# Seven block products for all of one feed-forward layer, and weight sums moved from DMA to VectorE

## The chip, the cores and the metric

The kernel runs on one core of a Trainium2 chip. The metric is the device time of one execution in microseconds (us). A core has TensorE (PE; its weight loads are shown apart as PEld), VectorE (DVE), ScalarE (ACT), GpSimd (POOL) and SyncE (SP), and 16 DMA engines that serve all queues. In this kernel SP issues nearly all loads and stores, and POOL issues DMAs that add one DRAM array to another and the gathers of the paged cache.

## The reference

The reference is one inference step of a two-layer decoder for 1024 prompt tokens and 8 sample tokens that share all weights. The width is 1024 and the feed-forward width `D_FF` is 2816. Layer 0 mixes tokens with a gated linear recurrence beside cross-attention into 256 memory tokens; layer 1 mixes them with stick-breaking attention (over keys and values projected once, after layer 0) beside the same kind of memory attention. Each layer ends with a SwiGLU feed-forward block, and a normalisation stands around every block:

```python
def swiglu(h, w_gu, w_down):
    gate, up = jnp.split(h @ w_gu, 2, axis=-1)
    return (jax.nn.silu(gate) * up) @ w_down

h = h + rmsnorm(mix, g[1])
h = h + rmsnorm(swiglu(rmsnorm(h, g[2]), w_gu[l], w_down[l]), g[3])
```

Everything is float32. The outputs are the activations of all tokens, the recurrence's states, and the new keys and values.

## The kernel before

**Tokens and tiles.** Activations lie transposed: 8 tiles of 128 features by the tokens. There are two token groups: group 0 has 512 prompt tokens, group 1 has 512 prompt tokens and the 8 sample tokens (520 columns, worked on as two halves of 260). "Second half" below means group 1. A float32 product is made as three products of rounded pieces: each weight tile and each activation is split into a high part (a cast on ACT, `split_w` L206 and `split` L501) and a low part (a subtraction on DVE, L207 and L502), and high by high, high by low and low by high are added in PSUM.

**Feed-forward.** `D_FF` is cut into 22 slices of 128, in five parts, `PARTS` = 5, 5, 4, 4, 4 slices. A part makes its slices (gate product, up product, SiLU, multiplication, split), and then the part's share of the down product for 8 blocks of rows, added to the result. The slices exist in three forms:

- `ffn.part` (L684): gate and up are two full products through `proj` (L220). For group 1 a slice is 2 x 8 x 3 x 2 = 96 matmuls of 260 columns. SiLU is made of exp, ln and exp on ACT (L238 to L240).
- `gate_up_q` (L452, "plain"): the same 96 matmuls into four single PSUM banks Q0 to Q3, while the generator `sums_w` (L279) makes sums and differences of the activations' blocks between them. These are on DVE, with a split on ACT and DVE after each.
- `gate_up_w` (L482, "seven products"): gate and up for two token halves are a 2 x 2 block product, made by a Winograd-form scheme with 7 block products instead of 8: 7 x 4 x 3 = 84 matmuls of 260 columns (L511). Its seven weight operands are four blocks of `w_gu` and three further sums of them. Between the products ACT copies a negated bank into the next one (L518, L521), so that the order pa, pd, pb, pa, pb, pc, pb of the banks matters.

The sums of weight blocks are made in DRAM ahead of use by `weight_sums` (L549): per part four arrays s1 to s4, in 16 steps (two row halves of eight), each a DMA from POOL's queue that copies (L568) or adds (L566). Ahead of each stands a one-column copy on POOL (L563) that waits for a recent result named by `now[0]`; it holds the DMA back to that point of the program.

Class `ffn_w` (L575) runs parts with `gate_up_w`; its first three slices are plain ones, in which the activation sums come about. Layer 0 group 1 uses `ffn.part` for parts 0 and 1 (10 slices) and `ffn_w` from part 2 on (3 plain, 9 with seven products). Layer 1 group 1, the last work of the kernel, uses `ffn_w` for all five parts (3 plain, 19 with seven products).

**Order.** The kernel's main line (from L1535 on) is a list of stages. `weave` interleaves generators by weights (how far each has come of its expected count of steps). A scheduler then puts the instructions of the built program into the order in which each engine issues them; engines take their own list strictly in that order. The stages named below, in the time of the profiled run:

- 185 to 290 us: group 0's recurrence beside the memory keys and values.
- 672 to 852 us: the rest of group 1's layer-0 mixer beside group 0's layer-0 feed-forward parts 2 to 4.
- 990 to 1209 us, called the attention stage here: `b0.sb` and `b0.mem` (group 0's layer-1 attention: 12 steps of stick-breaking and 8 of memory attention) beside parts 0 and 1 of group 1's layer-0 feed-forward. 34 steps of layer 1's weight sums run in it too.
- 1209 to 1404 us: parts 2 to 4 of that feed-forward, alone.
- 1600 to 1920 us: group 1's layer-1 attention, prompt and sample, beside group 0's layer-1 feed-forward.
- 2067 to 2407 us, called the final stage here: group 1's layer-1 feed-forward, beside group 0's last output in its first 60 us.

The attention writes its result into eight tiles `xo` (`wo_tiles`), as high and low parts (`split_to` at the end of `sb_prompt` and `mem_attn`); the output projection `o0.mm(b0.xo, ...)` reads them after the feed-forward of group 1 has ended.

**Buffers.** Raw weight tiles come from `wraw` (5), in seven-product parts by turns from other pools as well; split weights come from `wspl` (5), and in part from `cpool`. `tpool` has 3 tiles, `mpool` 5.

Of the kernel before, what the change touches and what calls it, by code (L numbers as in the profile page):

```python
# [18 lines left out]
P = 128  # L19
# [4 lines left out]
def tile_decoder(  # L24
# [204 lines left out]

    def silu(dst, ps, g):  # L230


        n = NG[g]
        x = T()
        dst = T() if dst is None else dst
        d = dst[:, :n]
        nc.vector.tensor_scalar(sv(x, g), pv(ps, g), -44.0, None, op0=ALU.max)  # L237
        nc.scalar.activation(d, x[:, :n], AF.Exp, scale=-1.0)  # L238
        nc.scalar.activation(d, d, AF.Ln, bias=1.0)
        nc.scalar.activation(d, d, AF.Exp, scale=-1.0)  # L240
        nc.vector.tensor_mul(d, d, x[:, :n])
        return dst
# [36 lines left out]
    def sums_w(g, xs, ops, YT, ZT):  # L279
# [5 lines left out]
        for k in range(4):  # L285
            x0, x1 = xs[k], xs[k + 4]
            y = YT()
            if k % 2 == 0:
                z, u = ZT(), ZT()
            o = (k % 2) * h  # L290
            ops.append([
                x0[:, :, :h], x1[:, :, :h], x1[:, :, h:n], z[:, :, o : o + h], u[:, :, o : o + h],
                y[:, :, :h], y[:, :, h : 2 * h],
            ])

            def full(x, c):
                t = B()
                nc.vector.tensor_add(t[:, :h], x[:, 0, c : c + h].bitcast(F32), x[:, 1, c : c + h].bitcast(F32))
                return t

            b11, b12, b21, b22 = full(x0, 0), full(x0, h), full(x1, 0), full(x1, h)
# [150 lines left out]
    def gate_up_q(g, l, f, xt, side, n_side, first):  # L452
# [4 lines left out]
        for j in range(2):  # L457
# [14 lines left out]
            for a in range(2):  # L472
                d = sg[:, a * h : (a + 1) * h]
                if j == 0:
# [7 lines left out]
    def gate_up_w(g, l, f, ops, spl, raws):  # L482
# [5 lines left out]
        src = [  # L488
# [16 lines left out]
        def product(ps, j, first=False):  # L505
            w = split(weight(j))
            i = src[j][1]
# [16 lines left out]
        nc.scalar.activation(sg[:, :h], pa[:, :h], AF.Silu)  # L524
        product(pb, 4)
        dt = T()
        nc.scalar.copy(dt[:, h:n], pd[:, :h])
        gt = T()
        nc.vector.tensor_add(gt[:, h:n], dt[:, h:n], pb[:, :h])
        product(pc, 5)  # L530
        nc.vector.tensor_sub(gt[:, :h], pc[:, :h], dt[:, h:n])
        product(pb, 6)
        act[0] = nc.scalar.activation(sg[:, h:n], gt[:, :h], AF.Silu)
# [41 lines left out]
    class ffn_w:  # L575


        def __init__(self, g, l, x, steps, first, rows, R=None, own=False):
# [3 lines left out]
            self.half = []  # L582

            def YT():
                if rows:
# [5 lines left out]
            self.sums = sums_w(g, x, self.ops, YT, YT if rows else lambda: A(F32R))  # L591

        def spl(self):
            self.n += 1
            if (self.pi or not self.rows) and not self.own and self.n % 8 in (1, 4, 6):
# [9 lines left out]
        def raws(self):  # L605
            self.r += 1
            if not self.rows and self.r % 2:
# [8 lines left out]
        def part(self, pi):  # L616
# [5 lines left out]
            for j in range(nf):  # L622
                self.pi = pi
                if f0 + j < self.plain:
                    mids.append(
                        gate_up_q(g, l, f0 + j, self.x, self.sums, self.steps[j], PARTS[self.first][0])
                    )
                    now[0] = mids[-1][:, 0, 0:1].bitcast(F32)
                else:
                    mids.append(gate_up_w(g, l, f0 + j, self.ops, self.spl, self.raws))  # L630
# [233 lines left out]
    def mem_attn(g, l, qm, xo):  # L864
# [4 lines left out]
        for h in range(H):  # L869
# [41 lines left out]
            d = xo[H + h]  # L911
            split_to((d[:, 0, :G], d[:, 1, :G]), po)
# [427 lines left out]
    def sb_prompt(g, Qs, xo):  # L1340
# [49 lines left out]
        for h in range(H):  # L1390
# [13 lines left out]
            d = xo[h]  # L1404
            split_to((d[:, 0, :G], d[:, 1, :G]), po)
# [18 lines left out]
    class mixer_b:  # L1424
# [7 lines left out]
        def open(self):  # L1432
            self.xo = wo_tiles(self.g)
# [41 lines left out]
    with tc.issue_after(made[0].ins):  # L1475
# [60 lines left out]
    weave((a0.fq(), 8), (mem_load(), 2))  # L1536
    weave(
        (a0.core(), 22),
# [5 lines left out]
    w0 = weight_sums(0, (3, 4, 2))  # L1544
    weave((a0.mem(), 8), (a1.fq(), 8), (islice(w0, 12), 13))
    o0 = out_proj(0, 0, M)
    drain(o0.mm(a0.xo))
    weave((o0.finish(), 17), (chain(a1.v(), a1.qm(A)), 8), (islice(w0, 12), 13))
    f0 = ffn(0, 0, o0.x)
    weave((a1.core(), 22), (f0.part(0), 9), (islice(w0, 16), 17))  # L1550
    a1.open()
    weave((a1.sample(), 6), (a1.gate(), 4), (f0.part(1), 9), (w0, 9))
    ws = weight_sums(1, range(5))
# [10 lines left out]
    weave((chain(a1.merge(), a1.mem()), 30), (a1.mem_sample(), 50), (rest(), 24), (islice(ws, 2), 6))  # L1564
# [8 lines left out]
    weave((b0.heads(), 8), (o1.finish(), 17), (islice(ws, 4), 4))  # L1573
# [13 lines left out]
    weave((kv_proj(1, xk1), 8), (islice(ws, 10), 11))  # L1587
    weave((normed(1, f1.R, f1.r, lambda k: gcol(1, 0, k), xb1), 8), (o0.mm(b0.xo, 7, ND), 1))
    b1 = mixer_b(1, xb1)
    weave((b1.heads(), 8), (o0.finish(), 17), (islice(ws, 8), 9))  # L1590
# [8 lines left out]
    weave((o1.mm(b1.xo), 8), (ws, 9))  # L1599
# [37 lines left out]
```

## Time and profile before

| | |
|---|---|
| median of 3 runs | 2450.82 us (2448.91 to 2453.11) |
| the profiled execution | 2446.43 us, its span 2444.6 us |
| granted TensorE clock | 0.999 |
| PE busy | 2412.0 us, 99% of the span, 15839 matmuls |
| DVE busy | 1639.0 us, 67% |
| ACT busy | 1251.2 us, 51% |
| POOL busy | 186.1 us, 8% |
| DMA | 397.42 MB, of it 79.70 MB by POOL's queue |

The profile page gives, in this order, busy time by engine, the span in 40 slices, DMA queues, the chain of work that ended last, the costliest groups of instructions and the DMA issues. A row of a group reads: line, engine, operation, output<-inputs, shape, count | busy us, mean ns of one | idle time before them and what ended it. A row of a window reads: the stretch, its length, and each engine's busy us with its count of instructions, then the clock, the mean busy share of the DMA engines and GB/s. A row of the timeline reads: start us, length us, engine, line, operation, count, and in brackets idle time before it. The length of a matmul in the rows is the time from its start to its modelled end; matmuls overlap, so that length isn't their spacing.

### The profile page before, as it was taken

Reading aid. Unit: us, or ns where it says so; the run is one execution under the profiler, and the core shown is the slowest. Engines: PE = TensorE matmul, PEld = TensorE weight load, DVE = VectorE, ACT = ScalarE, POOL = GpSimd, SP = SyncE. Lnnn points to the kernel's source line nnn. Section 1 sums busy time; section 2 is a strip of 40 time slices with the busy share of each in tenths; the row PEclk is TensorE's granted clock in tenths of the full one; section 3 lists DMA queues with packets and bytes.
Section 4 is the critical chain, followed back from the end, with each engine's and each line's share of the span. In section 5 each row is a group of like instructions: output and inputs, shape, how many; then the busy total and the mean of one; then the engine's idle time right before and its main releaser. Section 6 shows DMA issues by size and latency. Waiting matters only on the chain.

```text
span 2444.6 us, 42106 instructions
## 1 busy us (share of the span) xinstructions
PE 2412.0 (99%) x15839; PEld 2159.3 (88%) x15839; DVE 1639.0 (67%) x2987; ACT 1251.2 (51%) x2441; POOL 186.1 (8%) x315
## 2 busy tenths in 40 slices
PE   8999999999999999999999999999999999999998
PEld 6888888888889988999999989877777888999998
DVE  5867557665897686654756686777788467755565
ACT  5547544344445555554434554555555445654445
POOL 1001101101000000111200102121000100000000
PEclk9999999999999999999999999999999999999999
DMA  5454666577746447677766649655354563464542
GB/s 187 120 166 117 161 191 158 134 192 186 209 132 172 123 156 232 179 179 168 196 166 165 202 139 293 196 151 150 99 163 121 145 192 119 140 193 144 148 145 73
DMA packets 534734, 397.42 MB, mean 163 GB/s; under 512 B 21325, under 2 KB 473018, under 8 KB 534530
## 3 DMA queue, kind: packets, MB, share of 16 engines
q1 hardware_dynamic: 505346, 315.02, 43.3%
q0 software_dynamic: 29184, 79.70, 14.1%
q8 instruction: 125, 2.05, 0.3%
q14 instruction: 79, 0.65, 0.1%
HBM read 364.81 MB, written 101.14 MB: 191 GB/s over the span
## 4 chain that ended last, share of the span: by engine, by line
PE 87%; DVE 6%; DMA 3%; issue 2%; ACT 2%; POOL 0%; SPq 0%; DVEq 0%; ACTq 0%; POOLq 0%
PE mm L220 46%; PE q L511 13%; PE q L648 9%; PE q L464 3%; PE mm L1042 2%; PE s L1188 1%; PE s L906 1%; PE s L1385 1%; PE mm L851 1%; PE mm L824 1%; PE s L875 1%; PE q L680 1%; PE s L1351 1%; DVE ws L207 1%; DMA b<-qd 1%
## 5 line engine op out<-in xcount | busy, mean ns | idle before, releaser
L220 PE MATMUL mm<-x,ws 128*128 128x260 f32 (+1 forms) x6240 | 1115.6, 335 | 3.5 <-DVE r L657 1.7
L220 PEld LDWEIGHTS mm<-x,ws 128*128 128x128 f32 x6240 | 941.0, 188 | 123.9 <-DVE x L228 2.1
L206 ACT CAST ws<-w 128x512 fp32r<-128x512 f32 (+1 forms) x652 | 382.3, 588 | 492.1 <-PE mm L220 336.2
L207 DVE TENSOR_TENSOR ws<-w,ws 128x512 fp32r<-128x512 f32 (+1 forms) x652 | 418.6, 648 | 246.0 <-ACT ws L206 232.0
L220 PE MATMUL mm<-m,ws 128*128 128x512 f32 (+1 forms) x1344 | 281.8, 361 | 0.5 <-DVE r L400 0.4
L220 PEld LDWEIGHTS mm<-m,ws 128*128 128x128 f32 x1344 | 217.8, 188 | 37.2 <-issue 1.0
L648 PE MATMUL q<-m,ws 128*128 128x260 f32 (+1 forms) x1824 | 222.0, 282 | 0.0
L648 PEld LDWEIGHTS q<-m,ws 128*128 128x128 f32 x1824 | 219.0, 188 | 1.3 <-DVE t L534 0.7
L502 DVE TENSOR_TENSOR ws<-w,ws 128x512 fp32r<-128x512 f32 x181 | 124.0, 690 | 89.7 <-ACT ws L501 86.3
L501 ACT CAST ws<-w 128x512 fp32r<-128x512 f32 x181 | 111.8, 621 | 110.8 <-PE q L648 31.9
L511 PE MATMUL q<-x,ws 128*128 128x260 f32 (+1 forms) x1188 | 158.1, 282 | 0.0
L511 PEld LDWEIGHTS q<-x,ws 128*128 128x128 f32 x1188 | 148.7, 188 | 0.0
L511 PE MATMUL q<-y,ws 128*128 128x260 f32 x912 | 119.7, 283 | 0.4 <-ACT q L521 0.4
L511 PEld LDWEIGHTS q<-y,ws 128*128 128x128 f32 x912 | 113.6, 188 | 0.9 <-ACT q L521 0.6
L464 PE MATMUL q<-x,ws 128*128 128x260 f32 (+1 forms) x720 | 91.3, 284 | 0.2 <-DVE r L400 0.2
L464 PEld LDWEIGHTS q<-x,ws 128*128 128x128 f32 x720 | 88.4, 188 | 1.8 <-DVE r L400 0.5
L511 PE MATMUL q<-a,ws 128*128 128x260 f32 (+1 forms) x672 | 87.0, 282 | 0.0
L511 PEld LDWEIGHTS q<-a,ws 128*128 128x128 f32 x672 | 83.2, 188 | 0.0
L657 DVE TENSOR_TENSOR r<-r,q 128x260 f32<-128x260 f32 (+1 forms) x128 | 48.4, 420 | 48.2 <-PE q L648 48.1
L237 DVE TENSOR_SCALAR t<-mm 128x512 f32<-128x512 f32 (+1 forms) x58 | 40.0, 690 | 48.6 <-PE mm L220 48.4
L563 POOL COPY mk<-a 128x1 f32<-128x1 f32 x36 | 21.9, 609 | 640.4 <-ACT a L1241 392.1
L566 POOL DMA_DIRECT2D wsum<-in_w_gu x64 | 58.5, 935 | 114.1 <-DMA wsum<-wsum 89.5
(355 smaller groups left out, 3027.8 us busy)
## 6 DMA issues: line engine op xcount, KB each, us to landing
w<-in_w_gu SPq DMA_DIRECT2D x297, 256.0 KB
w<-in_w_down SPq DMA_DIRECT2D x160, 256.0 KB
wsum<-in_w_gu POOLq DMA_DIRECT2D x72, 512.0 KB, 6.5
w<-wsum SPq DMA_DIRECT2D x104, 256.0 KB
w<-in_w_in_a SPq DMA_DIRECT2D x80, 256.0 KB
w<-in_w_o SPq DMA_DIRECT2D x64, 256.0 KB
wsum<-in_w_gu POOLq DMA_DIRECT2D x24, 640.0 KB, 6.8
wsum<-wsum POOLq DMA_DIRECT2D x24, 512.0 KB, 5.6
```

Of the source, the lines that this page charges most:

```text
L206: nc.scalar.copy(ws[:, 0, :n, :], raw[:, :n, :])
L207: nc.vector.tensor_sub(ws[:, 1, :n, :], raw[:, :n, :], ws[:, 0, :n, :].bitcast(F32))
L220: nc.tensor.matmul(ps[:, a, : PW[g]], wt, xt[k][:, xi, o : o + PW[g]], start=(k == 0 and wi == 0), stop=(k == nk - 1 and wi == 2),)
L237: nc.vector.tensor_scalar(sv(x, g), pv(ps, g), -44.0, None, op0=ALU.max)
L464: ins = nc.tensor.matmul(pp[a][:, :h], wt, xt[k][:, xi, a * h : (a + 1) * h], start=(k == 0 and wi == 0), stop=(k == ND - 1 and wi == 2),)
L501: nc.scalar.copy(w[:, 0, :], src)
L502: nc.vector.tensor_sub(w[:, 1, :], src, w[:, 0, :].bitcast(F32))
L511: nc.tensor.matmul(ps[:, :h], w[:, wj, k * P : (k + 1) * P], x[:, xi, :], start=(first and k == 0 and wi == 0), stop=(k == 3 and wi == 2), ...
L566: nc.gpsimd.dma_start(d, a, accum_op=ALU.add)
L648: nc.tensor.matmul(pp[a][:, :h], wt, mids[k][:, xi, a * h : (a + 1) * h], start=(k == 0 and wi == 0), stop=(k == nf - 1 and wi == 2),)
L657: nc.vector.tensor_add(d, d, pp[a][:, :h])
L1042: nc.tensor.matmul(pb[i][:, a, :], xt[k][:, xi, c * P : (c + 1) * P], ws[:, s, :], start=(k == 0 and wi == 0), stop=(k == ND - 1 and wi == 2),
```

## The change

1. Group 1's layer-0 feed-forward uses `ffn_w` from part 0 on: 3 plain slices and 19 with seven products, where it had 13 slices of 96 matmuls and 9 of 84. Parts 0 and 1 still run beside `b0.sb` and `b0.mem`, now in a form called `lean`: SiLU is again exp, ln, exp (`gated`) over all 520 columns at once. In these parts the raw tiles come from `wraw` and the split ones from `wspl` alone. The sums of activations read the normalised activations (`src=o1.R`) and no longer add high and low parts first.
2. The weight sums of layer 0 cover all five parts, in the order 3, 4, 0, 1, 2 (80 steps; 48 before). They start with the first mixer: 14 steps in the stage at 185 us, then 8, 6, 8 and 4, 24 in the stage at 672 us, and the last 16 in the attention stage.
3. Layer 1's weight sums in DRAM (80 steps) are gone. `gate_up_w` without them loads the four blocks of `w_gu` and makes the sums in SBUF with four `tensor_add` on DVE (128x512) per slice.
4. `b0`'s attention output goes to a DRAM array (`put`: a copy on ACT and a store), since the tiles that held it now hold activation sums. `b0.load` reads it back and splits it beside the last down product of that feed-forward.

```diff
+    def put(xo, i, cols, src):
+        if isinstance(xo, list):
+            split_to((xo[i][:, 0, cols], xo[i][:, 1, cols]), src)
+            return
+        t = B()[:, : cols.stop - cols.start]
+        nc.scalar.copy(t, src)
+        nc.sync.dma_start(xo[:, i, cols], t)
...
+            if src:
+                b11, b12, b21, b22 = (src[i][:, c : c + h] for i in (k, k + 4) for c in (0, h))
+            else:
+                b11, b12, b21, b22 = full(x0, 0), full(x0, h), full(x1, 0), full(x1, h)
...
+    def gated(d, x):
+        nc.scalar.activation(d, x, AF.Exp, scale=-1.0)
+        nc.scalar.activation(d, d, AF.Ln, bias=1.0)
+        nc.scalar.activation(d, d, AF.Exp, scale=-1.0)
+        nc.vector.tensor_mul(d, d, x)
...
         def weight(j):
-            r = raws()
-            nc.sync.dma_start(r, src[j][0].rearrange("(k p) m -> p k m", p=P))
-            return r.rearrange("p k m -> p (k m)")
+            if src:
+                return load(src[j][0])
+            if j == 0:
+                for name, r, c in (("a11", 0, gate), ("a21", 0, up), ("a22", 512, up), ("a12", 512, gate)):
+                    raw[name] = load(w_gu[l][r : r + 512, c : c + P])
+            elif j == 1:
+                raw["s1"] = B()
+                nc.vector.tensor_add(raw["s1"], raw["a21"], raw["a22"])
+            elif j == 2:
+                nc.vector.tensor_add(raw["a21"], raw["a11"], raw["a21"])
+                raw["s2"] = B()
+                nc.vector.tensor_add(raw["s2"], raw["a21"], raw["a22"])
+            elif j == 5:
+                nc.vector.tensor_add(raw["s2"], raw["s2"], raw["a12"])
+            return raw[("a11", "s1", "s2", "a12", "a21", "s2", "a22")[j]]
...
+        if lean:
+            nc.vector.tensor_scalar(sg[:, :h], pa[:, :h], -44.0, None, op0=ALU.max)
...
+            nc.scalar.copy(dt[:, :h], pd[:, :h])
+            nc.vector.tensor_add(gt[:, h:n], dt[:, :h], pb[:, :h])
+            product(pc, 5)
+            nc.vector.tensor_sub(sg[:, h:n], pc[:, :h], dt[:, :h])
+            nc.vector.tensor_scalar(sg[:, h:n], sg[:, h:n], -44.0, None, op0=ALU.max)
+            x, sg = sg, T()
+            product(pb, 6)
+            gated(sg[:, :n], x[:, :n])
...
         nc.vector.tensor_mul(sg[:, :h], sg[:, :h], pb[:, :h])
         nc.vector.tensor_mul(sg[:, h:n], sg[:, h:n], gt[:, h:n])
...
+        def load(self):
+            d, n, self.xo = self.xo, NG[self.g], []
+            ts = []
+            for k in range(ND + 2):
+                if k < ND:
+                    ts.append(T()[:, :n])
+                    nc.sync.dma_start(ts[k], d[:, k, :n])
+                if k >= 2:
+                    x = X(self.g)
+                    split_to((x[:, 0, :n], x[:, 1, :n]), ts[k - 2])
+                    self.xo.append(x)
+                yield
...
+    w0 = weight_sums(0, (3, 4, 0, 1, 2))
     weave(
-        (a0.core(), 22),
+        (a0.core(), 22), (islice(w0, 14), 15),
...
-    weave((chain(a1.merge(), a1.mem()), 30), (a1.mem_sample(), 50), (rest(), 24), (islice(ws, 2), 6))
+    weave((chain(a1.merge(), a1.mem()), 30), (a1.mem_sample(), 50), (rest(), 24), (islice(w0, 24), 24))
...
-    b0.open()
-    f1 = ffn(1, 0, o1.x)
-    weave((chain(b0.sb(), b0.mem()), 25), (chain(f1.part(0), f1.part(1)), 18), (islice(ws, 34), 35))
-    set_banks(True)
-    fw = ffn_w(1, 0, o1.x, (5, 6, 5), 2, False, f1.R)
-    weave((chain(fw.part(2), fw.part(3), fw.part(4)), 24), (islice(ws, 8), 8))
-    f1.acc = fw.acc
+    b0.open(True)
+    set_banks(True)
+    fw = ffn_w(1, 0, o1.x, (5, 6, 5), 0, False, beside=(0, 1), src=o1.R)
+    weave((chain(b0.sb(), b0.mem()), 25), (chain(fw.part(0), fw.part(1)), 18), (w0, 60))
+    p4 = fw.part(4)
+    weave((chain(fw.part(2), fw.part(3), islice(p4, 4)), 20))
+    weave((p4, 4), (b0.load(), 10))
+    f1 = ffn(1, 0, o1.x)
+    f1.R, f1.acc = fw.R, fw.acc
```

More of the change, by code (lines that the diff above doesn't have):

```diff
@@ L575, in tile_decoder, with __init__ @@
     class ffn_w:
-        def __init__(self, g, l, x, steps, first, rows, R=None, own=False):
+        def __init__(self, g, l, x, steps, first, rows, R=None, own=False, beside=(), src=None):
             self.g, self.l, self.x, self.ops, self.steps, self.rows, self.own = g, l, x, [], steps, rows, own
@@ L589, in YT @@
                 return A(F32R)
-            self.sums = sums_w(g, x, self.ops, YT, YT if rows else lambda: A(F32R))
+            self.sums = sums_w(g, x, self.ops, YT, YT if rows or beside else lambda: A(F32R), src)
         def spl(self):
             self.n += 1
-            if (self.pi or not self.rows) and not self.own and self.n % 8 in (1, 4, 6):
+            if (self.pi or not self.rows) and not self.own and self.pi not in self.beside and self.n % 8 in (1, 4, 6):
                 return cpool.tile([P, 2, 512], F32R, tag="c", name=nm("ws"))
@@ L606, in raws @@
             self.r += 1
-            if not self.rows and self.r % 2:
+            if not self.rows and self.pi not in self.beside and self.r % 2:
+                return B().rearrange("p (k m) -> p k m", k=4)
+            if self.rows and not self.pi and self.r % 2:
                 return B().rearrange("p (k m) -> p k m", k=4)
```

81 lines of the change are left out of this document (47 added, 34 removed).

## The prediction

> **What bounds the kernel now.** I read the page first: the engines' busy time, the clock, and the chain that ended last.
>
> ```profile
> span 2444.6 us, 42106 instructions
> PE 2412.0 (99%) x15839; PEld 2159.3 (88%) x15839; DVE 1639.0 (67%) x2987; ACT 1251.2 (51%) x2441; POOL 186.1 (8%) x315
> ...
> PEclk9999999999999999999999999999999999999999
> ...
> PE 87%; DVE 6%; DMA 3%; issue 2%; ACT 2%; POOL 0%; SPq 0%; DVEq 0%; ACTq 0%; POOLq 0%
> ```
>
> PE is busy for 99% of the span at the full clock and makes 87% of the chain. So the time moves with what PE has to do, and with the waits that an edit adds to PE. VectorE is next, at 67%. A matmul's length is no price here, since matmuls overlap; their spacing is. The timeline and the groups by shape show it:
>
> ```profile
> 2211.33 29.04 PE L648 MATMUL q<-m,ws 128*128 128x260 f32 x240
> ...
> 1486.98 5.99 PE L220 MATMUL mm<-x,ws 128*128 128x260 f32 x48
> ...
> L511 PE MATMUL q<-y,ws 128*128 128x260 f32 x912 | 119.7, 283 | 0.4 <-ACT q L521 0.4
> ```
>
> One matmul of 260 columns is 283 ns long, but 240 in a row take 29.04 us: (29.04 - 0.28)/239 = 0.120 us from start to start. The L220 run gives (5.99 - 0.28)/47 = 0.121. I price each at 0.120 us.
>
> Third, windows by stage, for how full the other engines are where the change puts work:
>
> ```profile
> 185.00:290.00 105.00, 103.92 (x669) 92.72 (x669) 69.65 (x133) 72.63 (x162) 11.59 (x24) 1.00 0.47 121
> 672.00:852.00 180.00, 177.88 (x1334) 166.40 (x1333) 136.60 (x269) 91.83 (x193) 0.76 (x2) 1.00 0.49 144
> 948.00:1003.00 55.00, 55.00 (x302) 46.27 (x303) 42.36 (x74) 30.36 (x53) 4.91 (x7) 1.00 0.85 238
> 990.00:1209.00 219.00, 218.35 (x1691) 207.96 (x1691) 133.26 (x262) 113.52 (x230) 34.56 (x65) 1.00 0.70 174
> 1384.00:1404.00 20.00, 20.00 (x168) 19.83 (x166) 14.15 (x27) 8.83 (x14) 1.21 (x2) 1.00 0.69 190
> 1600.00:1920.00 320.00, 313.70 (x1472) 241.26 (x1472) 247.18 (x389) 167.32 (x328) 22.13 (x20) 1.00 0.44 132
> 2103.00:2125.00 22.00, 21.57 (x178) 21.12 (x177) 15.97 (x32) 13.96 (x31) 0.00 (x0) 1.00 0.73 213
> 2311.00:2344.00 33.00, 33.00 (x277) 33.00 (x277) 21.71 (x39) 19.60 (x40) 0.00 (x0) 1.00 0.61 176
> ```
>
> After the stage's length come PE, PEld, DVE, ACT and POOL, then the clock and the DMA engines' share. In the attention stage (990 to 1209) PE idles 0.65 us; in the final stage not at all; in the stage with the fullest VectorE beside attention (1600 to 1920, DVE 247/320 = 77%) it idles 6.3 us, 2.0%.
>
> **The change, part by part.**
>
> *Matmuls.* Ten slices go from 96 to 84 matmuls: 120 fewer. The built program agrees: 8184 matmuls of 260 columns instead of 8304, all else on PE the same in number. 120 x 0.120 = 14.4 us off PE: 7 slices x 12 x 0.120 = 10.1 in the attention stage, and 4.3 in the stage behind it, whose three plain slices become seven-product ones. The Trainium skill, page "TensorE: Matmul & The Clock Gate", section "Back-to-back issue gap", puts the spacing at N/2.4 + 2.5 ns, which is 111 ns at 260 columns; by it the sum below would lose 1.1 us of its gain. The rows above say 120, and I keep them.
>
> *Work beside attention.* What VectorE gains and loses there:
>
> ```profile
> L237 DVE TENSOR_SCALAR t<-mm 128x520 f32<-128x520 f32 x10 | 7.0, 698 | 12.3 <-PE mm L220 12.3
> L241 DVE TENSOR_TENSOR t<-t,t 128x520 f32<-128x520 f32 x10 | 7.0, 700 | 12.4 <-ACT t L240 12.4
> L716 DVE TENSOR_TENSOR t<-t,mm 128x520 f32<-128x520 f32 x10 | 7.0, 696 | 15.3 <-PE mm L220 15.3
> L298 DVE TENSOR_TENSOR b<-x 128x260 f32<-128x260 f32 x16 | 6.3, 419 | 0.0
> ...
> L502 DVE TENSOR_TENSOR ws<-w,ws 128x512 fp32r<-128x512 f32 x17 | 11.8, 691 | 7.8 <-ACT ws L501 7.7
> L228 DVE TENSOR_TENSOR m<-t,m 128x520 fp32r<-128x520 f32 x3 | 2.1, 700 | 0.0
> L531 DVE TENSOR_TENSOR t<-q,t 128x260 f32<-128x260 f32 x4 | 1.7, 428 | 0.1
> ```
>
> Off: ten times L237, L241 and L716 (20.9 us), the 16 additions L298 (6.7), the eight subtractions of the attention's output (5.5, moved to the load). On: a seven-product slice splits 7 weight tiles instead of 4, so 21 x 0.69 = 14.5; ten products of `gated` at 0.70 (7.0); 54 operations of 260 columns, four in a plain and six in a seven-product slice, at 0.42 (22.7); two half additions for one whole in part 1's down product (1.2). Net +12 us: 145.6 of 209 us, 70%. ACT gains 21 casts of 0.62, 21 bank copies of 0.37 and 1 us of down copies, +22 us: 65%. So neither is the bound, but the chains are longer: a split tile lasts 12 matmuls instead of 24, from five buffers, and SP loads 7 tiles a slice instead of 4. Between the stages with DVE at 61% (idle 0.3%) and 77% (idle 2.0%), 70% gives 1.3% of 209, some 2 us more than the 0.65 now. I take +3, with -1 (that idle gone, and a little spacing) and +10.5 (the chain of the second case below, unhidden) as ends.
>
> *Weight sums on VectorE, final stage.* By lengths a seven-product slice now has 7 x 0.691 + 0.70 + 4 x 0.42 = 7.2 us on DVE beside 84 x 0.120 = 10.1 on PE; four additions of 0.69 make it 10.0. That looks full, but lengths overlap here too:
>
> ```profile
> 1322.09 1.28 DVE L502 TENSOR_TENSOR ws<-w,ws 128x512 fp32r<-128x512 f32 x2
> ...
> 1320.43 0.76 DVE L657 TENSOR_TENSOR r<-r,q 128x260 f32<-128x260 f32 x2 [0.99 <-PE q L648]
> ```
>
> Two subtractions take 1.28, so the second comes 0.59 after the first; for 260 columns 0.34. By spacing a slice needs 11 x 0.60 + 0.6 + 4 x 0.34 = 8.6 of 10.1 us, 85%, and catches up in each down product. I take +0.5 for 17 slices, and +1 for the two behind the window 2103 to 2125, where DVE has 16.0 of 22 already and 5.5 more come. Lower end 0, upper end the third case. That loads fall from seven to four a slice gains nothing: PE doesn't wait there.
>
> *Sums by DMA.* POOL issues 48 adding or copying steps fewer over all, each moved past its queue's waiting one-column copies; nothing else stands behind these but the sample gathers, which come later.
>
> ```profile
> q1 hardware_dynamic: 505346, 315.02, 43.3%
> q0 software_dynamic: 29184, 79.70, 14.1%
> ```
>
> 128 steps took at most 14.1% of 2444.6 us of all 16 engines: 2.7 us each. Fourteen in the stage at 185 lift its DMA share from 0.47 to 0.83, 22 more in the stage at 672 from 0.49 to 0.82. The window 948 to 1003 has 0.85 and no PE idle, so I charge +0.5 in all; ends 0 and +3 (the 1.1 and 2.1 us that PE idles in these two stages, doubled). In the attention stage 18 steps go (49 us) and 21 loads and 8 stores of 256 KB come, at 0.433 x 2444.6 us / 315 MB some 0.9 us each (26 us): its 0.70 falls to about 0.6. Nothing is gained for it.
>
> *Hand-over.* Eight tiles are read back and split beside the last down product. Its window (1384 to 1404) has DVE at 14.15 of 20; 8 x 0.69 = 5.5 more in 23.3 us makes 94%. PE already waits there once:
>
> ```profile
> 1404.93 2.33 PE L220 MATMUL mm<-x,ws 128*128 128x512 f32 x9 [0.90 <-DVE r L657]
> ```
>
> +1, ends 0 and +5.5 if the splits hide nowhere.
>
> *Sum.* -14.4 + 3 + 1.5 + 0.5 + 1 = -8.4 us. The profiled execution took 2446.43 us, so it would take 2438; it lies 4.4 under the median of the three runs, and 2450.8 - 8.4 gives 2442 for the median.
>
> **Rivals.**
>
> *The SiLU chain in the attention stage eats the gain.* `gated` works on both halves at once, so bank pb stays taken until the whole chain behind product 5 is done, and the next slice's third product needs pb.
>
> ```profile
> L238 ACT ACTIVATE t<-t 128x520 f32<-128x520 f32 x10 | 6.4, 641 | 0.9
> L886 ACT ACTIVATE b<-s,nmx 128x256 f32<-128x256 f32 x16 | 7.5, 472 | 6.6 <-DVE nmx L880 6.6
> ...
> L501 ACT CAST ws<-w 128x512 fp32r<-128x512 f32 x16 | 9.9, 621 | 5.3 <-PE q L511 3.8 <-ACT ws L501 1.5
> ...
> L518 ACT ACTIVATE q<-q 128x260 f32<-128x260 f32 x3 | 1.1, 372 | 0.6 <-PE q L511 0.6
> ```
>
> Subtraction and maximum 0.85, three ACT passes 1.92 with a cast (0.62) and two attention exponentials (0.94) among them, two products 1.12, the negated copy 0.37: 5.8 us. PE has products 6, 0 and 1 meanwhile, 36 x 0.120 = 4.3. That is 1.5 us a slice, 10.5 for seven, and with 3 in the final stage and 2 elsewhere the sum is +1: 2452, no change. For it: these chains are built into the order. Against it: PE has attention matmuls to put in that place, and now loses 0.65 us in 219.
>
> *VectorE bounds the final stage (slower).* If additions can't overlap, a slice costs 10.0 us on DVE plus the waits for ACT that its row L502 shows, 7.8 us in 3.3 slices, 2.4 each: 12.3 against 10.1, 19 x 2.2 = +42, and 2450.8 - 14.4 + 42 + 4.5 = 2483. It decides once a slice's DVE time passes 10.1. The two rows of overlapping pairs speak against it. The Trainium skill has the rule for it, page "VectorE: DVE Perf Modes", section "The DRAIN you can't avoid": the next operation cannot issue until the pipe is empty. The trace agrees with its page's length for such an addition (691 ns) but not with the rule, with 0.59 us between starts.
>
> *The earlier sums starve the loads.* If an eighth of the DMA time that joins the two early stages (36 x 2.7 = 97 us) shows up on PE, 12 us come back: -8.4 + 12 = +4, 2455. For it: the steps are let go by one-column copies that wait for few results, so they may come in bursts. Against it: the window with a share of 0.85.
>
> **How the numbers follow.** Forecast 0.58 (own range 2434 to 2447), SiLU chain 0.22, VectorE 0.12, loads 0.08. A measurement of this kernel tells about 0.2%, 4.9 us, from no change. Faster (under 2446): most of the forecast, 0.56. Same: the rest of it and most of the SiLU chain, 0.22. Slower: VectorE, the loads, and the chain at its worst, 0.22. The range leaves out the full VectorE case: 2433 to 2460.
>
> **What would show it.** PE's busy time should fall by about 14 us and its share stay at 98 or 99%. Between `b0`'s first attention matmul and the first output projection the time should fall by 9 to 14. In the final stage DVE should rise to some 80% with PE full; PE idle ended by DVE ws L544 would show the third case, and PE idle ended by ACT at the negated copies the second. More PE idle ended by DMA in the first 850 us would show the fourth. The sum is wrong if PE idles in a place that I gave no price.

## The result and the profile after

The changed kernel takes 2469.95 us (median of 4 runs, 2465.35 to 2471.22) against 2451.97 us (2448.91 to 2453.52) before: a ratio of 1.0077, 95% interval 1.0066 to 1.0089. It is 18 us slower, where 2442 was forecast. From the page of the changed kernel: span, busy time, POOL's DMA queue, the chain that ended last.

```profile
span 2467.5 us, 41940 instructions
PE 2409.1 (98%) x15719; PEld 2152.9 (87%) x15719; DVE 1702.7 (69%) x3125; ACT 1278.1 (52%) x2517; POOL 137.2 (6%) x219
...
q0 software_dynamic: 19200, 54.53, 9.8%
...
PE 80%; DVE 8%; DMA 6%; issue 3%; ACT 2%; POOL 0%; SPq 0%; DVEq 0%; ACTq 0%; POOLq 0%
```

The matmuls are gone (15719 for 15839) and POOL moves 25 MB less, but PE has fallen from 87 to 80% of the chain and DMA has doubled from 3 to 6%. Where the 22.9 us of span arose is seen from three instructions of PE: the first attention matmul of `b0`, the first matmul of the output projection behind it, and the first of the final stage. The timeline of the kernel before (its second row stands in the prediction, at 1404.93), then of the changed one:

```profile
990.74 0.39 PE L1351 MATMUL s<-a,a 128*128 128x128 f32 x2
...
2073.19 0.41 PE L464 MATMUL q<-x,ws 128*128 128x260 f32 x2
```

```profile
1014.71 0.39 PE L1411 MATMUL s<-a,a 128*128 128x128 f32 x2
...
1425.29 0.47 PE L220 MATMUL mm<-x,ws 128*128 128x512 f32 x1 [0.83 <-DVE r L718]
...
2092.52 0.41 PE L481 MATMUL q<-x,ws 128*128 128x260 f32 x2
```

| stretch, us | before | after | difference |
|---|---|---|---|
| start to attention | 990.7 | 1014.7 | +24.0 |
| attention to output projection | 414.2 | 410.6 | -3.6 |
| to the final stage | 668.3 | 667.2 | -1.0 |
| final stage to the end | 371.4 | 375.0 | +3.6 |

All of the loss, and more, lies ahead of the attention stage. Up to there the two programs have the same order on PE, DVE, ACT and SP, but for a dozen operations of DVE and ACT in the last 5 us; only POOL's queue, with the weight sums, differs. Windows of that stretch, before and after (stretch, length, then busy us of PE, PEld, DVE, ACT, POOL with counts, clock, DMA share, GB/s):

```profile
110.00:134.00 24.00, 24.00 (x183) 22.41 (x181) 20.57 (x58) 7.66 (x13) 0.00 (x0) 1.00 0.56 180
...
735.00:852.00 117.00, 116.18 (x972) 115.31 (x971) 79.26 (x158) 59.92 (x117) 0.00 (x0) 1.00 0.53 152
```

```profile
110.00:134.00 24.00, 17.89 (x118) 15.76 (x118) 17.36 (x47) 6.10 (x11) 5.50 (x8) 0.95 1.06 273
...
672.00:735.00 63.00, 57.13 (x276) 44.98 (x275) 47.46 (x83) 26.14 (x62) 5.48 (x10) 0.95 0.71 184
735.00:852.00 117.00, 112.85 (x913) 110.64 (x912) 79.12 (x170) 61.26 (x127) 14.46 (x24) 0.99 0.77 203
```

The 14 steps meant for the stage at 185 us are issued from 91 to 129 us, since the results that their copies on POOL wait for are ready early (the last of these waits ends at 98.7 us): the DMA engines are full and PE does 118 matmuls where it did 183. The timeline shows how a late load reaches PE:

```profile
125.32 0.62 ACT L206 CAST ws<-w 128x512 fp32r<-128x512 f32 x1 [8.47 <-DMA w<-in_w_mem_kv]
130.26 1.35 ACT L206 CAST ws<-w 128x512 fp32r<-128x512 f32 x2 [4.33 <-DMA w<-in_w_mem_kv]
...
133.89 0.69 PE L893 MATMUL mm<-ident,t 128*128 128x128 f32 x2 [4.94 <-ACT t L890]
...
687.29 1.23 DVE L993 TENSOR_TENSOR c<-c,b 128x1024 f32<-128x1024 f32 x1 [2.58 <-DMA b<-qd]
...
692.02 1.22 PE L220 MATMUL mm<-m,ws 128*128 128x512 f32 x2 [3.95 <-DVE r L411]
...
790.98 0.62 ACT L543 CAST ws<-w 128x512 fp32r<-128x512 f32 x1 [7.02 <-DMA w<-wsum]
...
792.70 1.56 PE L709 MATMUL q<-m,ws 128*128 128x256 f32 x7 [3.77 <-DVE r L718]
```

Each time ACT or DVE stands in its queue behind one late tile, with work for others behind it, and PE's gap is named after that other work (`t`, `r`), not after the DMA. There is a second cost. Windows behind the gap at 692 us, and behind one of 2.44 us at 2190.9:

```profile
692.00:693.00 1.00, 0.98 (x2) 0.83 (x3) 1.00 (x3) 0.43 (x2) 0.64 (x2) 0.50 0.73 279
...
697.00:698.00 1.00, 1.00 (x4) 0.79 (x3) 0.41 (x1) 0.71 (x3) 0.00 (x0) 0.50 0.96 287
698.00:700.00 2.00, 2.00 (x10) 1.46 (x10) 1.09 (x3) 1.19 (x4) 0.00 (x0) 1.00 0.01 2
...
2191.00:2192.00 1.00, 1.00 (x9) 1.00 (x10) 1.00 (x3) 0.21 (x1) 0.00 (x0) 1.00 0.70 206
```

After 3.95 us without work PE is granted half the clock for 6 us; after 2.44 us the full one. The Trainium skill, page "TensorE: Matmul & The Clock Gate", section "Part 1: The HAM clock gate (the "warmup" mystery)", says that the clock falls to half after an idle window of some 3.4 us; these rows agree. Other runs here show that the length of a gap doesn't settle it: a gap of 2.25 us (run 5, ending at 552.8 us) is followed by half the clock and one of 3.45 us (run 4, ending at 1077.4 us) is not. In all 14 traces the times at which the clock changes lie whole multiples of 3.41 us apart. From 100 us on, each stretch of that grid at the full clock in which PE was busy for less than 0.45 of the time is followed by half the clock, each above 0.51 by the full one, and those between by either. So what counts here is how much of a gap falls into one such stretch.

### The profile page after: what moved, and what is told of

It reads as the page before. It is cut to its first block, busy times and chain, and to the rows that moved or that the text cites. A ratio compares the mean times of both kernels' runs of the same rounds, so it can differ in the third digit from the quotient of the medians.

```text
span 2467.5 us, 41940 instructions
## 1 busy us (share of the span) xinstructions
PE 2409.1 (98%) x15719; PEld 2152.9 (87%) x15719; DVE 1702.7 (69%) x3125; ACT 1278.1 (52%) x2517; POOL 137.2 (6%) x219
## 4 chain that ended last, share of the span: by engine, by line
PE 80%; DVE 8%; DMA 6%; issue 3%; ACT 2%; POOL 0%; SPq 0%; DVEq 0%; ACTq 0%; POOLq 0%
PE mm L220 39%; PE q L553 16%; PE q L709 9%; PE mm L1102 2%; PE q L481 2%; PE s L1445 1%; DVE ws L207 1%; PE s L1248 1%; DMA c<-in_cache_mem_v 1%; PE s L967 1%; PE s L1411 1%; PE q L741 1%; PE s L936 1%; PE mm L885 1%; DMA c<-vd 1%
## 5 line engine op out<-in xcount | busy, mean ns | idle before, releaser
L220 PE MATMUL mm<-x,ws 128*128 128x512 f32 (+1 forms) x5280 | 990.1, 344 | 4.8 <-DVE r L718 1.7
L220 PEld LDWEIGHTS mm<-x,ws 128*128 128x128 f32 x5280 | 822.6, 188 | 124.3 <-issue 2.7
L206 ACT CAST ws<-w 128x512 fp32r<-128x512 f32 x612 | 357.4, 586 | 450.1 <-PE mm L220 280.3
L207 DVE TENSOR_TENSOR ws<-w,ws 128x512 fp32r<-128x512 f32 x612 | 392.0, 646 | 249.9 <-ACT ws L206 240.3
L709 PE MATMUL q<-m,ws 128*128 128x260 f32 (+1 forms) x2304 | 287.6, 284 | 6.1 <-DVE r L718 5.8
L553 PE MATMUL q<-y,ws 128*128 128x260 f32 x1824 | 244.5, 284 | 3.0 <-DVE t L585 2.4
L553 PEld LDWEIGHTS q<-y,ws 128*128 128x128 f32 x1824 | 228.8, 188 | 4.7 <-DVE t L585 2.7
L220 PE MATMUL mm<-m,ws 128*128 128x512 f32 x864 | 222.0, 405 | 4.0 <-DVE r L411 3.9
L544 DVE TENSOR_TENSOR ws<-w,ws 128x512 fp32r<-128x512 f32 x180 | 123.6, 689 | 67.5 <-ACT ws L543 66.3
L543 ACT CAST ws<-w 128x512 fp32r<-128x512 f32 x180 | 111.0, 620 | 84.3 <-PE q L553 26.6
L543 ACT CAST ws<-b 128x512 fp32r<-128x512 f32 x121 | 74.7, 620 | 68.8 <-PE q L709 33.4
L544 DVE TENSOR_TENSOR ws<-b,ws 128x512 fp32r<-128x512 f32 x121 | 83.1, 689 | 29.2 <-ACT ws L543 28.5
L227 ACT CAST m<-t 128x512 fp32r<-128x512 f32 (+1 forms) x88 | 54.9, 624 | 23.9 <-DVE t L777 12.3
```

Of the source, the lines that this page charges most:

```text
L206: nc.scalar.copy(ws[:, 0, :n, :], raw[:, :n, :])
L207: nc.vector.tensor_sub(ws[:, 1, :n, :], raw[:, :n, :], ws[:, 0, :n, :].bitcast(F32))
L220: nc.tensor.matmul(ps[:, a, : PW[g]], wt, xt[k][:, xi, o : o + PW[g]], start=(k == 0 and wi == 0), stop=(k == nk - 1 and wi == 2),)
L227: nc.scalar.copy(dst[0], src)
L543: nc.scalar.copy(w[:, 0, :], src)
L544: nc.vector.tensor_sub(w[:, 1, :], src, w[:, 0, :].bitcast(F32))
```

## The experiments

Theory A: the bytes that POOL's sums move ahead of the attention stage make loads late. Theory B: the loss comes from the steps as such (copies, issues) or from the other parts of the change. All times below are medians; the kernel before had 2448.7 to 2449.4 us on the same chips. Losses at a place are the lateness of the same matmul against the kernel before, in the profiled executions.

**1. Early steps that move little.** The changed kernel, without the sums of parts 0 to 2 (their products read plain blocks of `w_gu` instead):

```diff
...
-                d, a = (v[256 * (i // 8) : 256 * (i // 8) + 256] for v in (d, a))
+                nr = 256 if f0 >= 14 else 16
+                d, a = (v[256 * (i // 8) : 256 * (i // 8) + nr] for v in (d, a))
```

> The changed kernel, in which each of the 48 weight-sum steps of layer 0's parts 0, 1 and 2 moves 16 rows in place of 256, and the loads of those sums read blocks of `w_gu` of the same size (so the sums of these parts are left out). Order of all instructions as before this edit. Theory A, the sums' DMA volume starves the loads: the 24 us lost by 990 us come back, and the gaps of 0.9 and 3.5 us in the attention stage with them: 2441 to 2448 us. Theory B, the loss comes from the steps themselves (a copy on POOL and an issue each) or from the other parts of the change, whatever is moved: 2465 to 2471 us.

Measured: 2445.61 us, ratio 0.9984 (0.9975 to 0.9994). 24 us come back with the same steps and copies, so A. By 990 us it is still 8.5 us late, nearly all of it by 150 us: the first 14 steps belong to part 3 and kept their size.

**2. The early steps alone, in the kernel before.**

```diff
-    w0 = weight_sums(0, (3, 4, 2))
+    w0 = weight_sums(0, (3, 4, 0, 1, 2))
...
-        (a0.core(), 22),
+        (a0.core(), 22), (islice(w0, 14), 15),
...
-    weave((chain(a1.merge(), a1.mem()), 30), (a1.mem_sample(), 50), (rest(), 24), (islice(ws, 2), 6))
+    weave((chain(a1.merge(), a1.mem()), 30), (a1.mem_sample(), 50), (rest(), 24), (islice(w0, 24), 24))
...
```

> The kernel before, with nothing changed but POOL's steps: layer 0's sums cover five parts in the changed kernel's order and pace (64 steps by 990 us where 54 stood, 14 of them in the stage at 185 us and 24 in the one at 672 us), and layer 1's steps move back by as much. Theory A: the loss by 990 us is as in the changed kernel, some 24 us, and 2472 to 2478 us in all. Theory B: 2450 to 2456 us, the kernel before and a little for layer 1's later steps.

Measured: 2503.73 us, 1.0215 (1.0190 to 1.0241). Span against span it is 62 us late: 23.3 by 990 us, as in the changed kernel, and nothing in the attention stage, with 34 steps there as before. The other 38 were not foreseen, and the whole is far above the 2472 to 2478 us of theory A. They arise where layer 1's steps, moved behind that stage, stand closer: 7.6 us from 1209 to 1475 us (24 steps for 8) and 31 from 1490 to 1560 us in the time of the kernel before (24 steps for 18 from 1475 us on). The DMA engines are full there too (a share of 1.05 from 1520 to 1540 us of this run), and a second wait shows, in the list of waits from 1500 to 1640 us of this run (who waited for whom, us, times, longest): DVE may not overwrite a tile until POOL's one-column copy has read it, and POOL stands behind its own DMAs.

```profile
DVE t L1317 <- POOL mk L563: 23.4, 4, 8.4
```

**3. Layer 1's sums by VectorE alone**, in the kernel before.

```diff
+            elif j == 1:
+                raw["s1"] = B()
+                nc.vector.tensor_add(raw["s1"], raw["a21"], raw["a22"])
...
-    ws = weight_sums(1, range(5))
...
```

> The kernel before with part 3 of the change alone: layer 1's weight sums by VectorE, its 80 steps gone. By the prediction's term (+1.5) 2451 to 2455 us. If VectorE bounds the final stage, 2480 us or more. If the 80 steps did cost time where they stood, which no view of the kernel before shows, 2444 to 2450 us.

Measured: 2451.13 us, 1.0005 (0.9995 to 1.0014). The first line of the expectation holds in the time, as the sum of two effects: the final stage takes 377.4 us for 371.4, four times the term of +1.5, and the stretch ahead of it 666.1 for 668.3, where steps are gone. So the 80 steps did cost about 2 us in the kernel before. Of the 6.0 us a single gap of PE is 3.05, and 3.4 us of half clock follow it.

**4. The same volume later.** The changed kernel, with layer 0's parts 0 to 2 summed from 852 us on:

```diff
-        (a0.core(), 22), (islice(w0, 14), 15),
+        (a0.core(), 22),
...
-    weave((chain(a1.merge(), a1.mem()), 30), (a1.mem_sample(), 50), (rest(), 24), (islice(w0, 24), 24))
+    weave((chain(a1.merge(), a1.mem()), 30), (a1.mem_sample(), 50), (rest(), 24))
...
-    drain(kv_proj(0, xk0))
+    weave((kv_proj(0, xk0), 8), (islice(w0, 10), 11))
...
```

> The changed kernel with the 32 steps of parts 3 and 4 at the pace of the kernel before (12, 12, 8 from 290 us on) and the other 48 from 852 us on: 10 beside the keys and values, 8 beside the heads, 30 in the attention stage. The volume is the same. If what counts is which loads the steps meet (the stages before 852 us load a new weight tile every 24 matmuls of 512 columns or more often, and whole cache pages): no loss by 852 us, up to 8 us behind it, 2449 to 2457 us. If each step costs the same wherever it stands: 2466 to 2472 us.

Measured: 2464.03 us, 1.0059 (1.0038 to 1.0080), between both expectations and in neither. No loss by 852 us, as foreseen; but 10.5 us by the attention stage, and the stretch from there to the output projection takes 417.4 us. Moving the steps moved most of the loss with them: against run 6 below some 22 us are left of 28.

**5. Half steps.** The changed kernel; the same bytes at the same places, in two pieces each:

```diff
-            for i, (d, a, add) in enumerate(2 * (
+            for i, (d, a, add) in enumerate(4 * (
...
-                d, a = (v[256 * (i // 8) : 256 * (i // 8) + 256] for v in (d, a))
+                d, a = (v[128 * (i // 8) : 128 * (i // 8) + 128] for v in (d, a))
...
```

> The changed kernel with each weight-sum step cut into two of 128 rows: 160 steps where there were 80, two at each place, the same volume at the same time. If a step's size does the harm (a load that is issued behind one waits for the whole of it), half or more of the 24 us comes back: 2456 to 2462 us. If it is the volume that meets the loads at that time: 2466 to 2472 us. If POOL's copies and issues cost by themselves: above 2473 us.

Measured: 2450.32 us, 1.0002 (0.9992 to 1.0011): 20 us are back, more than was foreseen. By the profiled executions 13.0 of the 24 lost ahead of the attention stage are, and 4.7 from there to the output projection. Windows of this run:

```profile
110.00:134.00 24.00, 24.00 (x182) 22.41 (x182) 19.38 (x52) 7.67 (x13) 13.17 (x31) 1.00 1.05 275
...
735.00:852.00 117.00, 114.64 (x952) 113.07 (x951) 80.53 (x166) 62.86 (x127) 29.87 (x57) 1.00 0.85 224
```

From 110 to 134 us the DMA engines are as full as in the changed kernel (1.05 and 1.06, 275 and 273 GB/s), and PE loses nothing. So the share alone doesn't decide. Two things differ there. One step is over sooner, and POOL's queue has less of the engines, since an addition waits for the step before it in the same array: the same steps come from 91 to 182 us instead of 91 to 129. POOL's queue from 100 to 135 us, in the changed kernel and here (packets, MB, share of the 16 engines):

```profile
q0 software_dynamic: 2317, 5.70, 71.0%
```

```profile
q0 software_dynamic: 1788, 4.07, 53.8%
```

At the start no run here tells size from pace. From 672 to 870 us the pace is nearly the same and the size is what differs. POOL's queue there and its DMA issues with their median time to landing, of the changed kernel, of this one, and of run 9 below:

```profile
q0 software_dynamic: 4269, 13.37, 30.1%
...
wsum<-in_w_gu POOLq DMA_DIRECT2D x14, 640.0 KB, 8.0
```

```profile
q0 software_dynamic: 4695, 13.76, 31.8%
...
wsum<-in_w_gu POOLq DMA_DIRECT2D x31, 320.0 KB, 5.6
```

```profile
q0 software_dynamic: 4733, 12.12, 29.6%
...
wsum<-in_w_gu POOLq DMA_DIRECT2D x56, 160.0 KB, 4.7
```

The loss from 672 to 852 us is 13.7, 7.1 and 3.1 us in the three. It is made of a few gaps in one execution each, and size isn't all: from 510 to 560 us half steps lose more than whole ones, 3.5 us for 1.6.

The loads that PE's operands come from are late as well. From 100 to 135 us the median time from issue to the last of a load's 16 completion marks, taken from the trace for the 11 to 15 weight loads there, is 3.1 us before, 11.9 in the changed kernel, 5.4 with half steps. From 672 to 870 us it is 3.1, 4.9 and 5.1, with a longest of 5.8, 9.1 and 7.9: there the median is no better with half steps, only the longest wait. The longest gap of PE behind the start falls from 4.9 to 2.3 us, and the mean granted clock rises from 0.995 to 0.998. The Trainium skill, page "Perfetto Trace Analysis", section "DMA Optimizations", advises splitting DMAs where the engines are generally idle; here it gained 20 us where their share was 0.7 to 1.06 in the changed kernel.

**6. The change without the added DMA.** The changed kernel with the edit of run 1, and no steps in the stage at 185 us; the sums of parts 0 to 2 are left out.

> The changed kernel with the steps of parts 3 and 4 where the kernel before has them (12, 12, 8, none in the stage at 185 us) and the 48 others cut to 16 rows of 256 each, as in the first of these experiments (their sums are left out). What is left of the change is all but the added DMA. The prediction's sum without its term for the sums is -14.4 + 3 + 1.5 + 1 = -8.9 us: 2438 to 2443 us if these terms were right. From the first experiment, whose start still held 14 early steps of full size and was 8.5 us late by 990 us: 2436 to 2439 us. If the seven-product slices beside attention cost more than their term: 2446 us or more.

Measured: 2438.98 us, 0.9955 (0.9940 to 0.9970): 10.4 us faster, where the prediction's other terms make -8.9. Its page and timeline:

```profile
span 2437.8 us, 41930 instructions
PE 2399.3 (98%) x15719; PEld 2144.9 (88%) x15719; DVE 1703.0 (70%) x3125; ACT 1278.3 (52%) x2517; POOL 130.7 (5%) x219
```

```profile
991.38 0.39 PE L1415 MATMUL s<-a,a 128*128 128x128 f32 x2
...
1376.25 0.62 ACT L227 CAST x<-t 128x512 fp32r<-128x512 f32 x1 [5.46 <-DMA t<-xo]
...
1377.98 2.29 PE L713 MATMUL q<-m,ws 128*128 128x260 f32 x15 [3.18 <-DVE r L722]
...
1397.08 0.47 PE L220 MATMUL mm<-x,ws 128*128 128x512 f32 x1 [0.83 <-DVE r L722]
...
2063.47 0.41 PE L481 MATMUL q<-x,ws 128*128 128x260 f32 x2
```

PE's busy time is 9.8 us under the changed kernel's for the same 15719 matmuls, and its idle time (span less busy) 38.5 us for 58.4. So of the 29.7 us between the two spans 19.9 are gaps and 9.8 are slower matmuls. The clock fits: ahead of the last 10 us the changed kernel has four stretches at half the clock, 20.5 us in all (from 131.4, 691.2, 793.6 and 1087.1 us on), half of which is 10.2, and this run has none. A third of the price of late loads is the clock behind the gaps.

**7 and 8. Versions that compute all with half of the added sums.** Layer 0's DRAM sums for parts 3, 4, 1 and two slices of part 0; part 2 by VectorE. In the second, layer 1's first two slices with seven products also take DRAM sums.

```diff
-        src = None if l not in sums else [
+        if part == 0:
+            o -= 3 * P
+        src = None if part not in sums.get(l, {}) else [
...
-    w0 = weight_sums(0, (3, 4, 0, 1, 2))
+    w0 = weight_sums(0, (3, 4, 1, 0))
...
+    weave((chain(b0.sb(), b0.mem()), 25), (chain(fw.part(0), fw.part(1)), 18), (w0, 40))
...
```

> A version that computes all: the changed kernel with DRAM sums of layer 0 for parts 3, 4 and 1 at the pace of the kernel before (12, 12, 16, 8), for the two slices of part 0 that use sums in 16 steps of 256x256 (4, 6 and 6), and part 2's four slices with sums by VectorE. Theory A (volume that meets loads): the kernel before had 48 such steps at these places and lost nothing, so 2438 to 2444 us, faster than before by 0.2% or more. If the gain of the change is not there even without the added DMA: 2448 us or more.

> The version before, and layer 1's first two slices with seven products take their sums from DRAM again (16 steps of 256x256, 8 beside the keys and values, 8 beside the heads). The gap of 1.2 to 3.0 us that every run with VectorE's sums shows at the start of the final stage should go: 1 to 3 us less than the version before it. If that gap is not from the additions: the same time, or up to 2 us more.

Measured: 2447.96 us, 0.9991 (0.9982 to 1.0000), and 2448.14 us, 0.9988 (0.9979 to 0.9998). The first lies between its two lines, the second on its second line. By 990 us the first loses 1.2 us against run 6, as foreseen, but 6 us more at 1044, where the last whole steps stand directly ahead of the slices that use them and PE waits 3.3 us. In the second the gap at the start of the final stage stays (1.8 us), so DRAM sums for those slices don't remove it. Its timeline shows why:

```profile
2168.23 0.69 DVE L534 TENSOR_TENSOR b<-w,w 128x512 f32<-128x512 f32 x1 [2.29 <-DMA w<-in_w_gu]
...
2172.92 0.39 PE L555 MATMUL q<-y,ws 128*128 128x260 f32 x1 [1.80 <-DVE t L587]
```

The first addition of a slice (the fourth that VectorE sums in this stage) waits for a raw tile; then DVE runs without a pause until the addition L587 comes 4 us later, and PE waits for that. So the gap starts with a load that comes late, and what DVE has queued behind it makes it longer.

**9. Quarter steps.** The changed kernel with 320 steps of 64 rows:

```diff
-            for i, (d, a, add) in enumerate(2 * (
+            for i, (d, a, add) in enumerate(8 * (
...
-                d, a = (v[256 * (i // 8) : 256 * (i // 8) + 256] for v in (d, a))
+                d, a = (v[64 * (i // 8) : 64 * (i // 8) + 64] for v in (d, a))
...
```

> The changed kernel with each weight-sum step cut into four of 64 rows (320 steps), at the same places. If the harm goes with the bytes that a load finds in flight ahead of it, the loss between 560 and 870 us halves again (13.7 us with whole steps, about 10 of them left behind the start with half steps, then 4 to 6): 2442 to 2446 us. If half steps only helped by the pause that POOL makes between steps, or if 320 copies and issues cost by themselves: 2448 to 2456 us.

Measured: 2454.98 us, 1.0023 (1.0012 to 1.0033), in the range of the second line. But until 852 us the first held: 3.7 us late against the kernel before, where half steps are 10.8 and whole ones 23.9. Then 12.5 us are lost from 852 to 900 us by the wait seen in run 2:

```profile
878.54 1.42 DVE L392 SCALAR_TENSOR_TENSOR r<-r,par,st 128x512 f32<-128x512 f32 x2 [7.17 <-POOL mk L619]
```

POOL, which waits at each addition for the step before it, has fallen behind, and its copies still have to read the result `r` that DVE is to overwrite. A kernel with copies of other tiles there wasn't tried.

**10 to 12. Half steps in the versions that compute all.** Parts 3, 4 and 1 at the places of the kernel before, part 0's two slices done ahead of the attention stage; part 2 by VectorE (first), by DRAM in the attention stage (second), and the first with no steps from 510 to 670 us (third).

```diff
-    weave((a1.core(), 22), (f0.part(0), 9), (islice(w0, 8), 9))
+    weave((a1.core(), 22), (f0.part(0), 9), (islice(w0, 32), 34))
...
-    weave((chain(a1.merge(), a1.mem()), 30), (a1.mem_sample(), 50), (rest(), 24), (islice(w0, 24), 24))
+    weave((chain(a1.merge(), a1.mem()), 30), (a1.mem_sample(), 50), (rest(), 24), (islice(w0, 20), 24))
...
-    weave((b0.heads(), 8), (o1.finish(), 17))
+    weave((b0.heads(), 8), (o1.finish(), 17), (islice(w0, 12), 12))
...
```

> A version that computes all: sums of layer 0 in half steps, parts 3, 4 and 1 at the places of the kernel before, the two slices of part 0 that use sums all before the attention stage (20 and 12 steps of 128x256), part 2's four slices with sums by VectorE. The rest of the change cost 2439 us without added DMA; 1 to 2 for part 2's additions, 0 to 2 for the narrow steps: 2439 to 2443 us. If part 2's additions stall as those of the first slices in the final stage do (2 to 3 us once): 2443 to 2446 us.

> The version before, with part 2's sums from DRAM too, in 32 half steps spread over the attention stage. 2439 us and 0 to 2 for the narrow steps, and nothing for the attention stage, which took 405.9 us with 32 half steps and 405.7 without: 2438 to 2442 us. If part 2's sums come too late for its slices: 2444 us or more.

> The version with half steps and VectorE's sums for part 2, in which the stage from 510 to 670 us holds no steps: its 16 are divided between the stage before (40 for 32) and the one behind (28 for 20). In that stage the recurrence's state loads (DVE waits 3.5 us for one) are late by 5.6 us at 560 us against the run without the added steps, of which 3.0 are left at the end. If the steps that stand beside them do that: 3 us less, 2439 to 2441 us. If the stage behind loses as much with eight more: no change, 2443 us.

Measured: 2443.15 us, 0.9975 (0.9966 to 0.9984), which beats both kernels, at the border of its two lines; 2450.55 us, 1.0007 (0.9998 to 1.0016), as its second line says; 2443.71 us, 0.9976 (0.9966 to 0.9986), no change, so its second line too. In the second some 8 us are lost at 1209 us, where part 2 starts and ACT waits 6.29 us for a load beside the last steps. In the third the steps put ahead of 510 us run on to 529, PE has a gap of 2.6 us up to 530, and the stage behind loses 1.4 us more.

## Why the prediction was wrong

The step that failed is *Sums by DMA*: "I charge +0.5 in all; ends 0 and +3". It measured 24.0 - 0.6 = 23.4 us ahead of the attention stage, and 4.9 in it (410.6 for 405.7 us in run 6), where the last 16 steps were set off against 34 others that go. Three reasons of it fell:

- "The window 948 to 1003 has 0.85 and no PE idle." The changed kernel and run 5 have the same share in one window (1.06 and 1.05), one with a loss and one without. A mean share says how much is moved, not how late one load can come.
- The 14 steps were placed by their stage in the program. They wait only for results that are ready by 99 us, came 56 to 94 us ahead of that stage, in a burst, and met loads that no row of the sum spoke of.
- The upper end, twice the idle time seen, was taken from stages in which nothing was late. They say nothing of how long a gap gets once a load is late (3.5 to 4.9 us here), nor of the clock behind it.

The fourth rival named mechanism and place, bursts included, but had its price at half of what came (12 us for 23), and a chance of 0.08 on the strength of that same window. Its sign, PE idle ended by DMA in the first 850 us, didn't come in that form: no wait of PE there is put to a DMA. The profile names ACT (4.94 us) and DVE (3.95 and 3.77), and the DMA one step back, at the casts and additions that ACT and DVE wait with.

The other terms came out near, in part by luck. By run 6 against the kernel before, span against span (6.8 us apart, since the profiled execution of the kernel before lies some 3 us under its medians): attention to output projection 405.7 - 414.2 = -8.5, where -14.4 + 3 + 1 = -10.4 was forecast; final stage 374.3 - 371.4 = +2.9 for +1.5; -1.9 between them, unpriced, where layer 1's steps are gone. So the terms for the first and the last of these were 1.9 and 1.4 us too low, and a gain that stands in no term makes up for more than half. The -8.5 lies just outside the 9 to 14 us that the prediction gives for that stretch. PE's busy time falls by 2412.0 - 2399.3 = 12.7 of the 14 us named.

- Attention stage (+3) and hand-over (+1): together nearly 6. Of it the hand-over has 3.2 in one gap: ACT waits 5.46 us for the first tile read back (run 6), and the additions of the down product stand behind the splits on DVE. The step priced DVE's work there; what came late was the load.
- SiLU chain, second rival: not seen. The stretch gains 8.5 us without the added DMA, and no wait of PE in it (run 6, 4.8 us in four gaps) is ended by a negated copy.
- Weight sums on VectorE (+1.5): +2.9 in run 6, +6.0 in run 3. The term priced DVE's spare time in two windows; what came was a gap of 1.8 to 3.05 us behind one raw tile that lands late (runs 3 and 8). The prediction also says that PE idles not at all in this stage before; its row 2103 to 2125 has 0.43 us.
- VectorE as the bound, third rival: not seen. Over the final stage of the changed kernel (2092.5 to 2430 us) DVE is at 252.2 of 337.5 us, 75% where some 80% was forecast, and PE idles 3.6 us. From 2195 to 2235 us PE is full with DVE at 70%:

```profile
2195.00:2235.00 40.00, 40.00 (x334) 39.83 (x334) 28.20 (x52) 22.30 (x47) 0.00 (x0) 1.00 0.32 92
```

- The rule that the prediction sets against this rival's overlap: the same section of the Trainium skill, page "VectorE: DVE Perf Modes", section "The DRAIN you can't avoid", adds that an operation that isn't held starts earlier. So the 0.59 us between starts don't contradict that section.

## What to carry to other kernels

Price a DMA that is moved by how late it can make the next load that an in-order engine waits for, not by the mean share of the engines: read how long one such DMA takes to land, when its release really comes, and what stands behind the waiting cast or addition. Try background DMAs in pieces about as large as the loads they run beside (here 256 to 320 KB beside loads of 256 KB; pieces of half that made the issuing queue fall behind), and look at the waits of the queue that issues them: a copy that only holds a DMA back also holds the tile that it reads. When PE's busy time doesn't fall with its matmuls, look at the granted clock behind its gaps.

## What the runs showed of the hardware

- At the same DMA share (1.05 and 1.06) and GB/s (275 and 273) PE lost 0 or 6.1 us in 24 us, with background steps of 256 or 512 KB that held 54 or 71% of the engines' time. With background steps of 160, 320 and 640 KB that held 30 to 32% of it from 672 to 870 us it lost 3.1, 7.1 and 13.7 us. What in the DMA engines makes a load late beside such a step, no run here shows.
- Gaps of 3.5 to 4.9 us on PE in the changed kernel are each followed by a clock of 0.50; the gap of 2.44 us isn't. Over all runs gaps of 2.0 to 3.5 us fall on both sides, by how much of them falls into one stretch of a grid of 3.41 us. A third of the loss was the clock, not the gaps.
- VectorE's operations of 0.68 us start 0.60 apart when nothing holds them, additions and subtractions in turn. The timeline of the changed kernel behind its late tile at 2186 us:

```profile
2187.39 0.68 DVE L534 TENSOR_TENSOR w<-w,w 128x512 f32<-128x512 f32 x1
2187.99 0.68 DVE L538 TENSOR_TENSOR b<-b,w 128x512 f32<-128x512 f32 x1
2188.59 0.68 DVE L544 TENSOR_TENSOR ws<-w,ws 128x512 fp32r<-128x512 f32 x1
2189.19 0.68 DVE L536 TENSOR_TENSOR b<-w,w 128x512 f32<-128x512 f32 x1
```

A sum of lengths overstates VectorE's work by that much: 0.68 us each where 0.60 are used.
